# Second feed-forward matmul of a fused block: five groups by seven products and one plain, two groups interleaved, differences of activations formed in the first matmul

## Chip, cores and metric

The kernel runs on one core of one Trainium2 chip. The metric is the device time of one execution in microseconds (us). Before the change the median of three runs is 813.99 us (813.52 to 814.81).

## What is computed

One layer of a hybrid encoder block on 512 positions of 1024 features. The part that matters here is its end, the feed-forward network (in the kernel everything is float32, and every product of two float32 matrices is made of three TensorE matmuls on high and low parts):

```
xn = modulate(rmsnorm(h, norm2_g[l]), sh2, sc2)
ff = jnp.square(jax.nn.relu(xn @ w_ff1[l])) @ w_ff2[l]     # 512x1024 @ 1024x4096, then 512x4096 @ 4096x1024
h = h + g2[:, None, :] * ff
...
return rmsnorm(h, final_g)
```

## The kernel before, in words

**Tiles.** The hidden activations (after squared ReLU) stay in SBUF, feature-major, in tiles `hq[n, nh, th]` of 128 partitions x 512 elements: group `n` of 512 hidden features (8 groups), half `nh` of its features, half `th` of the 512 positions. In the code `a11 = hq[n,0,0]`, `a12 = hq[n,1,0]`, `a21 = hq[n,0,1]`, `a22 = hq[n,1,1]`. The second weight matrix comes in tiles of 128 x 1024 (512 KB): `F11`, `F21` (left half of the output features) through the feed `left`, `F12`, `F22` (right half) through the feed `right` (class `Feed`, L1041). Each feed has a fixed number of buffers: three for `left`, four for `right`. SyncE (SP) issues every load, in order, and a load waits until its buffer is free (L1053).

**Products.** The first matmul (L1013 to L1030) works on groups 1 to 7 with seven products each; a product there is 24 matmuls of 256 columns. The second matmul takes groups 0 to 5 in products (a product: 12 matmuls of 512 columns), and the last 8 of the 32 blocks of 128 features plainly (L1242 to L1259, 192 matmuls). `GROUPS = "WWSWWS"` says which of the six groups is of kind W (seven products, Winograd's form of Strassen's scheme) and which of kind S (eight plain products). The products run in two passes over the six groups: in the first a W group gives P1, P2, P7, P3 and an S group P2, P3, P2, P3; in the second a W group P5, P6, P4 and an S group P4, E, P4, E. That makes 24 + 20 = 44 products, numbered 0 to 43 here. P1 and P2 need tiles of `left` only; P7 and P3 are the first to need `right`. The accumulators take all eight PSUM banks, and `after` (L1171) adds them into SBUF tiles at products 20, 25 and 41.

**Operands.** Each product needs its weights split into high and low parts (`w_pair`, L1068: a ScalarE cast, L1075, and a VectorE subtraction, L1076, both on 128 x 1024) and its activations split (`hl`, L1084: ScalarE L1092, VectorE L1093, 128 x 512). A W group also needs differences of weights (VectorE, 128 x 1024: L1106, L1114, L1118, L1122) and of activations (VectorE, 128 x 512: `S3 = a11 - a21` in a tile of its own, L1105, then L1108 to L1110 in place). `passes` (L1096) is a generator that emits this work; `prefetch_step(5)` (L1197) keeps it five products ahead in program order. Split weights lie in five buffers, three of a pool that the first matmul uses too and two (`wx`) in the pool `passes`.

**Order.** The program order is a priority: a scheduler puts each engine's instructions in a fixed order ahead of time and may move one up into time in which it expects the engine to be free. The pools for `wx`, for `right` and for the split activations from the third on (`hsp`) take the room of the first matmul's operands, and so open only when its last product is done (L1143 to L1151). The first instruction that SyncE issues behind that point is the load of `fing` (L1147), the final norm's weights broadcast to all partitions, needed only at L1268. `gated` (L1165, two VectorE instructions a call) multiplies results by `g2` and adds them to the residual: quarter "1" at product 29 (L1209), the others through the list `late` (L1221) in the plain part, two calls per block.

Of the kernel before, what the change touches and what calls it, by code (L numbers as in the profile page):

```python
# [8 lines left out]
F32 = mybir.dt.float32  # L9
# [40 lines left out]
def block_kernel(ctx, tc, vecs_d, rows_d, ws_d, x_d, w_ada, w_in, w_out, w_ff1, w_ff2, out_d):  # L50
# [961 lines left out]

    for n in range(1, NB):  # L1013
# [16 lines left out]
        relu2(c12, c12)  # L1030

    GROUPS = "WWSWWS"
# [63 lines left out]
    def passes():  # L1096
        for pas in range(2):
            for n, kind in enumerate(GROUPS):
                a11, a12, a21, a22 = hq[n, 0, 0], hq[n, 1, 0], hq[n, 0, 1], hq[n, 1, 1]
                if kind == "W" and pas == 0:  # L1100
                    yield hl(a11), w_pair(left.get(), left)
                    yield hl(a12), w_pair(left.get(), left)
                    b12, b22 = right.get(), right.get()
                    s3 = fp.tile([P, 2, 256], F32, tag="tmp", name=f"S3{n}", bufs=2)
                    dve.tensor_sub(out=s3, in0=a11, in1=a21)  # L1105
                    dve.tensor_sub(out=b12, in0=b22, in1=b12)  # L1106
                    yield hl(s3), w_pair(b12, right)
                    dve.tensor_add(out=a21, in0=a21, in1=a22)  # L1108
                    dve.tensor_sub(out=a11, in0=a21, in1=a11)
                    dve.tensor_sub(out=a12, in0=a12, in1=a11)  # L1110
                    yield hl(a12), w_pair(b22, right)
                elif kind == "W":
# [3 lines left out]
                    yield hl(a21), w_pair(b12)  # L1116
# [3 lines left out]
                    yield hl(a11), w_pair(b22)  # L1120
# [10 lines left out]
    plan_ = [(pas, key) for pas in range(2) for kind in GROUPS for key in later(kind, pas)]  # L1131
# [15 lines left out]
    sp.dma_start(out=fing, in_=rows_d[5].partition_broadcast(P))  # L1147
# [48 lines left out]
    for i, (pas, key) in enumerate(plan_):  # L1196
        prefetch_step(5)  # L1197
        (h_, l_), (wh, wl) = ready.pop(0)
        first = (key, 0) not in acc_b
        for t in range(2):  # L1200
            if first:
                acc_b[key, t] = bank(f"g{key}{t}")
            ts_ = slice(t * P, (t + 1) * P)
            for j in range(2):
                mm3(acc_b[key, t], h_[:, j, ts_], l_[:, j, ts_], wh[:, j], wl[:, j], first and j == 0,
                    i == last_of[key] and j == 1 and key not in ("P4", "E"))
        for key_ in jobs.get(i, ()):
            after(key_)
        if i == end0 + 6:  # L1209
            for t in range(2):  # L1210
                gated("1", t, t, 0)
        if NS - i <= 4:
            ws_ff.prefetch(max(0, 4 - (NS - i)))
        if i == NS - 2:
            hs_pair(KF // 2)
# [5 lines left out]
    late = [(nm, t, row + t, hf) for nm, row, hf in (("3", 0, 1), ("7", 2, 0), ("5", 2, 1)) for t in range(2)]  # L1221
# [105 lines left out]
```

## Time and profile before

| | us |
|---|---|
| median of three runs | 813.99 |
| the profiled execution, its own time | 815.62 |
| its span, first to last instruction | 813.8 |
| TensorE busy | 795.4 (98%) |
| VectorE busy | 615.3 (76%) |
| ScalarE busy | 404.1 (50%) |
| mean granted TensorE clock | 0.994 of full speed |

The span is 1.8 us shorter than the execution's time. Busy TensorE counts modelled ends of pipelined matmuls: a matmul of 512 columns is shown as 0.39 us, while the next one starts 0.23 us after it. Likewise VectorE instructions overlap a little, so that the distance from start to start is what an instruction costs in a queue.

### The profile page before, as it was taken

How to read it: one execution, taken by the hardware profiler on the slowest of the kernel's cores; microseconds unless marked ns; L12 is line 12 of the kernel's file. 1: busy time of each engine (PE TensorE's matmuls, PEld its weight loads, DVE VectorE, ACT ScalarE, POOL GpSimd, SP SyncE). 2: the span in 40 equal slices, each digit the busy share in tenths (PEclk: the TensorE clock that was granted, in tenths of full speed). 3: DMA queues.
4: the chain of work that ended last, by engine and by line, in shares of the span. 5: the costliest groups of instructions: out<-in, count | busy, mean ns of one | idle time of the engine just before them, and what ended most of it. 6: DMA issues, size and time to landing. Idle time of an engine off the chain costs nothing.

```text
span 813.8 us, 11472 instructions
## 1 busy us (share of the span) xinstructions
PE 795.4 (98%) x4375; PEld 689.1 (85%) x4375; DVE 615.3 (76%) x925; ACT 404.1 (50%) x606; POOL 43.0 (5%) x62
## 2 busy tenths in 40 slices
PE   7999999999999999999999999999999799999996
PEld 6787888888988888888888899999999688888885
DVE  5889667684834367988756689988888898998936
ACT  5457556274432333242443446666666665555414
POOL 2004020121100000100000100000000000000000
PEclk9999999999999999999999999999999999999999
DMA  8974331143233398577345241333331676774302
GB/s 271 264 224 126 114 101 45 27 135 99 79 103 82 108 352 283 154 254 272 126 137 200 78 131 52 104 105 104 105 104 52 221 244 203 236 224 138 125 6 103
DMA packets 76423, 119.87 MB, mean 147 GB/s; under 512 B 5712, under 2 KB 38608, under 8 KB 76368
## 3 DMA queue, kind: packets, MB, share of 16 engines
q1 hardware_dynamic: 76368, 119.14, 46.0%
q8 instruction: 34, 0.56, 0.3%
q14 instruction: 21, 0.17, 0.1%
HBM read 117.02 MB, written 2.10 MB: 146 GB/s over the span
## 4 chain that ended last, share of the span: by engine, by line
PE 93%; DMA 2%; SPq 1%; ACT 1%; issue 1%; DVE 1%; POOLq 0%; POOL 0%
PE P L119 6%; PE P L117 6%; PE P L118 6%; PE gP L117 5%; PE gP L118 5%; PE gP L119 5%; PE qk L282 4%; PE wo L117 2%; PE wo L119 2%; PE wo L118 2%; PE f10b L118 1%; PE f10b L117 1%; PE f10b L119 1%; PE k1b L117 1%; PE o0b L119 1%
## 5 line engine op out<-in xcount | busy, mean ns | idle before, releaser
L1092 ACT CAST hsh<-h 128x512 fp32r<-128x512 f32 x38 | 23.6, 621 | 35.3 <-PE gP L118 27.2
L117 PE MATMUL gP<-wh_g,hsh 128*128 128x512 f32 x92 | 36.2, 396 | 0.2 <-ACT wh_g L1075 0.2
L118 PE MATMUL gP<-wl_g,hsh 128*128 128x512 f32 x92 | 35.8, 389 | 0.0
L119 PE MATMUL gP<-wh_g,hsl 128*128 128x512 f32 x92 | 35.8, 389 | 0.0
L1075 ACT CAST wh_g<-F 128x1024 fp32r<-128x1024 f32 x27 | 28.2, 1049 | 13.7 <-issue 7.1
L1076 DVE TENSOR_TENSOR wl_g<-F,wh_g 128x1024 fp32r<-128x1024 f32 x27 | 32.9, 1222 | 2.6 <-ACT wh_g L1075 2.5
L921 ACT CAST wh_T<-T 128x1024 fp32r<-128x1024 f32 x21 | 22.0, 1048 | 20.8 <-PE P L118 19.1
L118 PE MATMUL P<-x2l,wh_B 128*128 128x256 f32 x112 | 31.6, 282 | 0.0
L117 PE MATMUL P<-x2h,wh_B 128*128 128x256 f32 x112 | 31.6, 282 | 0.0
L119 PE MATMUL P<-x2h,wl_B 128*128 128x256 f32 x112 | 31.6, 282 | 0.0
L921 ACT CAST wh_B<-B 128x1024 fp32r<-128x1024 f32 x21 | 22.0, 1048 | 16.4 <-PE P L118 15.4
L1093 DVE TENSOR_TENSOR hsl<-h,hsh 128x512 fp32r<-128x512 f32 x38 | 25.9, 688 | 4.6 <-ACT hsh L1092 4.6
L117 PE MATMUL gP<-wh_x,hsh 128*128 128x512 f32 x60 | 23.8, 400 | 4.8 <-ACT wh_x L1075 4.8
L922 DVE TENSOR_TENSOR wl_T<-T,wh_T 128x1024 fp32r<-128x1024 f32 x21 | 25.7, 1224 | 2.6 <-ACT wh_T L921 2.5
L922 DVE TENSOR_TENSOR wl_B<-B,wh_B 128x1024 fp32r<-128x1024 f32 x21 | 25.6, 1220 | 0.0
L96 DVE TENSOR_TENSOR wl_gb<-raw_gb,wh_gb 128x1024 fp32r<-128x1024 f32 x8 | 9.8, 1224 | 19.7 <-ACT wh_gb L95 19.6
L118 PE MATMUL gP<-wl_x,hsh 128*128 128x512 f32 x60 | 23.7, 396 | 0.0
L119 PE MATMUL gP<-wh_x,hsl 128*128 128x512 f32 x60 | 23.6, 393 | 0.0
L667 DVE SCALAR_TENSOR_TENSOR accg<-arg,c_act,accg 128x1024 f32<-128x1024 f32 x14 | 18.0, 1283 | 5.6 <-DMA arg<-in_w_ada 5.5
L95 ACT CAST wh_ga<-raw_ga 128x1024 fp32r<-128x1024 f32 x8 | 8.4, 1051 | 27.2 <-PE ga0b L119 16.3
L1076 DVE TENSOR_TENSOR wl_x<-F,wh_x 128x1024 fp32r<-128x1024 f32 x17 | 20.7, 1222 | 1.4 <-ACT wh_x L1075 1.4
L118 PEld LDWEIGHTS P<-x2l,wh_B 128*128 128x128 f32 x112 | 21.3, 191 | 0.0
(610 smaller groups left out, 2815.5 us busy)
## 6 DMA issues: line engine op xcount, KB each, us to landing
F<-in_w_ff SPq DMA_DIRECT2D x48, 512.0 KB, 4.2
B<-in_w_ff SPq DMA_DIRECT2D x28, 512.0 KB, 3.8
ar<-in_w_ada SPq DMA_DIRECT2D x64, 128.0 KB, 3.4
arg<-in_w_ada SPq DMA_DIRECT2D x16, 512.0 KB, 5.9
raw_f<-in_w_ff SPq DMA_DIRECT2D x12, 512.0 KB, 3.3
raw_o<-in_w_in SPq DMA_DIRECT2D x8, 512.0 KB, 4.2
raw_mv<-in_w_in SPq DMA_DIRECT2D x8, 512.0 KB, 3.6
raw_gb<-in_w_in SPq DMA_DIRECT2D x8, 512.0 KB, 3.6
```

The source lines that it names most:

```text
L96: dve.tensor_sub(out=wl, in0=raw, in1=wh.bitcast(F32))
L117: pe.matmul(out, lhsT=ah, rhs=bh, start=start, stop=False)
L118: pe.matmul(out, lhsT=ah, rhs=bl, start=False, stop=False)
L119: pe.matmul(out, lhsT=al, rhs=bh, start=False, stop=stop)
L282: pe.matmul(bk, lhsT=wx[:, kk, f * P:(f + 1) * P], rhs=xx[k], start=k == 0 and ps_ == 0, stop=k == KT - 1 and ps_ == 2)
L667: dve.scalar_tensor_tensor(out=acc, in0=raw, scalar=c_act[:, k:k + 1], in1=acc, op0=ALU.mult, op1=ALU.add)
L921: act.copy(out=wh, in_=src)
L922: dve.tensor_sub(out=wl, in0=src, in1=wh.bitcast(F32))
L1075: act.copy(out=wh, in_=src)
L1076: dve.tensor_sub(out=wl, in0=src, in1=wh.bitcast(F32))
L1092: act.copy(out=h_, in_=src)
L1093: dve.tensor_sub(out=l_, in0=src, in1=h_.bitcast(F32))
```

## The change

The diff does the following. Group 2 becomes a W group (`GROUPS = "WWWWWS"`), which gives 43 products. The first pass begins with P1, P2 of group 0 and P1, P2 of group 1, then P7, P3 of both; the later groups keep their order. `a21` is replaced by `a11 - a21` beside the first matmul (`minus_a21`, one VectorE instruction for each of the five W groups), and the other differences of the activations are rewritten for it: three in the second matmul in place of four. The load of `fing` moves from the start of the second matmul to the last product of the first pass (`end0`, product 23). The `gated` calls of quarter "1" move into `late`.

```diff
@@ -1010,6 +1010,13 @@
         prefetch_op(2)
         return bk.rearrange("p (f t) -> p f t", f=2)
 
+    GROUPS = "WWWWWS"
+
+    def minus_a21(n):
+        if GROUPS[n:n + 1] == "W":
+            dve.tensor_sub(out=hq[n, 0, 1], in0=hq[n, 0, 0], in1=hq[n, 0, 1])
+
+    minus_a21(0)
     for n in range(1, NB):
         c = {(nh, th): ring(f"h{n}{nh}{th}") for nh in range(2) for th in range(2)}
         for key, v in c.items():
@@ -1028,8 +1035,8 @@
         relu2(c21, c21)
         dve.tensor_add(out=c12, in0=c12, in1=product(sum_op("S4"), f"P3{n}"))
         relu2(c12, c12)
-
-    GROUPS = "WWSWWS"
+        minus_a21(n)
+
     NF = len(GROUPS)
     NK = FF // P
     KF = 4 * NF
@@ -1094,30 +1101,32 @@
         return h_, l_
 
     def passes():
+        for n in range(2):
+            for nh in range(2):
+                yield hl(hq[n, nh, 0]), w_pair(left.get(), left)
         for pas in range(2):
             for n, kind in enumerate(GROUPS):
                 a11, a12, a21, a22 = hq[n, 0, 0], hq[n, 1, 0], hq[n, 0, 1], hq[n, 1, 1]
                 if kind == "W" and pas == 0:
-                    yield hl(a11), w_pair(left.get(), left)
-                    yield hl(a12), w_pair(left.get(), left)
+                    if n > 1:
+                        yield hl(a11), w_pair(left.get(), left)
+                        yield hl(a12), w_pair(left.get(), left)
                     b12, b22 = right.get(), right.get()
-                    s3 = fp.tile([P, 2, 256], F32, tag="tmp", name=f"S3{n}", bufs=2)
-                    dve.tensor_sub(out=s3, in0=a11, in1=a21)
                     dve.tensor_sub(out=b12, in0=b22, in1=b12)
-                    yield hl(s3), w_pair(b12, right)
-                    dve.tensor_add(out=a21, in0=a21, in1=a22)
-                    dve.tensor_sub(out=a11, in0=a21, in1=a11)
-                    dve.tensor_sub(out=a12, in0=a12, in1=a11)
+                    yield hl(a21), w_pair(b12, right)
+                    dve.tensor_sub(out=a21, in0=a22, in1=a21)
+                    dve.tensor_sub(out=a12, in0=a12, in1=a21)
+                    dve.tensor_add(out=a11, in0=a21, in1=a11)
                     yield hl(a12), w_pair(b22, right)
                 elif kind == "W":
                     b11, b12 = left.get(), right.get()
                     dve.tensor_sub(out=b12, in0=b12, in1=b11)
                     left.more()
-                    yield hl(a21), w_pair(b12)
+                    yield hl(a11), w_pair(b12)
                     b22 = right.get()
                     dve.tensor_sub(out=b22, in0=b22, in1=b12)
                     right.more()
-                    yield hl(a11), w_pair(b22)
+                    yield hl(a21), w_pair(b22)
                     b21 = left.get()
                     dve.tensor_sub(out=b21, in0=b21, in1=b22)
                     right.more()
@@ -1128,7 +1137,9 @@
                         yield x_, w_pair(left.get(), left)
                         yield x_, w_pair(right.get(), right)
 
-    plan_ = [(pas, key) for pas in range(2) for kind in GROUPS for key in later(kind, pas)]
+    plan_ = [(0, key) for key in ("P1", "P2") * 2 + ("P7", "P3") * 2]
+    plan_ += [(0, key) for kind in GROUPS[2:] for key in later(kind, 0)]
+    plan_ += [(1, key) for kind in GROUPS for key in later(kind, 1)]
     gen = passes()
     ready = []
 
@@ -1144,7 +1155,6 @@
     mhs.close()
     hsp = ff.enter_context(tc.tile_pool(name="hsp", bufs=1, side="right"))
     fing = hsp.tile([P, D], F32, name="fing")
-    sp.dma_start(out=fing, in_=rows_d[5].partition_broadcast(P))
     ps_stack = ExitStack()
     pass_pool.append(ps_stack.enter_context(tc.tile_pool(name="passes", bufs=1, side="right")))
     for _ in range(4):
@@ -1206,9 +1216,8 @@
                     i == last_of[key] and j == 1 and key not in ("P4", "E"))
         for key_ in jobs.get(i, ()):
             after(key_)
-        if i == end0 + 6:
-            for t in range(2):
-                gated("1", t, t, 0)
+        if i == end0:
+            sp.dma_start(out=fing, in_=rows_d[5].partition_broadcast(P))
         if NS - i <= 4:
             ws_ff.prefetch(max(0, 4 - (NS - i)))
         if i == NS - 2:
@@ -1218,7 +1227,7 @@
     lwp = ff.enter_context(tc.tile_pool(name="lwp", bufs=1, side="right"))
     o_banks = [[bank(f"ob{t}{hf}") for hf in range(2)] for t in range(2)]
     o_banks += [[acc_b["P4", t], acc_b["E", t]] for t in range(2)]
-    late = [(nm, t, row + t, hf) for nm, row, hf in (("3", 0, 1), ("7", 2, 0), ("5", 2, 1)) for t in range(2)]
+    late = [(nm, t, row + t, hf) for nm, row, hf in (("1", 0, 0), ("3", 0, 1), ("7", 2, 0), ("5", 2, 1)) for t in range(2)]
 
     def ff2_piece(k, last=False):
         if last:
```

## Rows read from the trace of the kernel before

**Rows 1.** The page of the profile: the line of busy times (engine, busy us, share of the span, instructions) and the first line of the chain that ended last.

```profile
PE 795.4 (98%) x4375; PEld 689.1 (85%) x4375; DVE 615.3 (76%) x925; ACT 404.1 (50%) x606; POOL 43.0 (5%) x62
...
PE 93%; DMA 2%; SPq 1%; ACT 1%; issue 1%; DVE 1%; POOLq 0%; POOL 0%
```

**Rows 2.** Waits of TensorE in the stretch 560 to 815 us: who waited for whom, us in total, times, longest. These are all it has there.

```profile
PE gP L117 <- ACT wh_x L1075: 4.8, 1, 4.8
...
PE gP L117 <- ACT wh_g L1075: 0.2, 1, 0.2
```

**Rows 3.** Table by stretches of the second feed-forward matmul (us from the span's start: length, busy us and instructions of PE, weight loads, DVE, ACT, POOL; granted clock; DMA share; GB/s).

```profile
641.60:646.50 4.90, 0.19 (x1) 0.00 (x0) 3.45 (x5) 1.99 (x3) 0.00 (x0) 1.00 0.77 295
...
651.00:702.00 51.00, 51.00 (x226) 42.24 (x226) 44.99 (x51) 30.46 (x38) 0.00 (x0) 1.00 0.68 225
...
702.00:762.70 60.70, 60.70 (x269) 50.26 (x269) 56.77 (x67) 31.11 (x38) 0.00 (x0) 1.00 0.56 179
```

**Rows 4.** The same table in stretches of 1 us behind the pause.

```profile
648.00:649.00 1.00, 1.00 (x4) 0.71 (x3) 1.00 (x2) 0.92 (x2) 0.00 (x0) 0.50 0.84 238
...
651.00:652.00 1.00, 1.00 (x6) 0.80 (x6) 1.00 (x3) 0.43 (x1) 0.00 (x0) 1.00 0.96 340
```

**Rows 5.** Timeline of TensorE (start us, length, engine, line, operation, tiles; in brackets the idle time before it): the first matmul of product 0, the last one before the pause, the first one behind it, the first and the last matmul of the plain part (192 matmuls).

```profile
636.16 0.40 PE L117 MATMUL gP<-wh_g,hs 128*128 128x512 f32 x1
...
641.40 0.39 PE L119 MATMUL gP<-wh_g,hs 128*128 128x512 f32 x1
...
646.55 0.77 PE L117 MATMUL gP<-wh_x,hsh 128*128 128x512 f32 x2 [4.76 <-ACT wh_x L1075]
...
762.81 0.39 PE L117 MATMUL ob<-wh_f,hsh 128*128 128x512 f32 x1
...
806.10 0.39 PE L119 MATMUL gE<-wh_f,hsl 128*128 128x512 f32 x1
```

**Rows 6.** The chain of waits of the stretch 600 to 700 us, in order of time (start us, us, what).

```profile
636.36 0.84 SPq L1147
...
637.25 7.24 DMA F<-in_w_ff
...
644.51 1.35 ACT wh_x L1075 x2
...
646.41 1.05 ACT wh_g L1075
```

**Rows 7.** Timeline of SyncE's queue: the last load issued before that of `fing`. Then the transfers issued in two short stretches, of that load (635.6 to 635.8 us) and of `fing` (636.2 to 636.4 us); the last number is us from issue to landing.

```profile
635.74 0.37 SPq L1053 DMA_DIRECT2D F<-in_w_ff  x1
...
F<-in_w_ff SPq DMA_DIRECT2D x1, 512.0 KB, 4.8
...
fing<-in_rows SPq DMA_DIRECT2D x1, 512.0 KB, 6.8
```

**Rows 8.** Timeline of VectorE around the pause.

```profile
640.03 0.68 DVE L1093 TENSOR_TENSOR hsl<-h,hsh 128x512 fp32r<-128x512 f32 x1
...
640.63 0.69 DVE L1093 TENSOR_TENSOR hsl<-S,hsh 128x512 fp32r<-128x512 f32 x1
...
644.58 1.22 DVE L1106 TENSOR_TENSOR F<-F,F 128x1024 f32<-128x1024 f32 x1 [1.45 <-DMA F<-in_w_ff]
...
650.26 1.22 DVE L1106 TENSOR_TENSOR F<-F,F 128x1024 f32<-128x1024 f32 x1
...
651.39 0.69 DVE L1093 TENSOR_TENSOR hsl<-h,hsh 128x512 fp32r<-128x512 f32 x1
```

**Rows 9.** Groups of instructions by line in 636.2 to 763 us (shapes, count, busy us, mean ns of one, idle before and its releaser): three of VectorE, one of ScalarE.

```profile
L1076 DVE TENSOR_TENSOR wl_g<-F,wh_g 128x1024 fp32r<-128x1024 f32 x25 | 30.5, 1222 | 2.3 <-ACT wh_g L1075 2.2
...
L1093 DVE TENSOR_TENSOR hsl<-h,hsh 128x512 fp32r<-128x512 f32 x32 | 21.9, 688 | 4.6 <-ACT hsh L1092 4.6
...
L1114 DVE TENSOR_TENSOR F<-F,F 128x1024 f32<-128x1024 f32 x4 | 4.9, 1223 | 0.5 <-DMA F<-in_w_ff 0.5
...
L1075 ACT CAST wh_g<-F 128x1024 fp32r<-128x1024 f32 x25 | 26.1, 1049 | 11.8 <-issue 7.1 <-DVE F L1106 2.7 <-PE gP L119 2.1
```

**Rows 10.** The end of the first feed-forward matmul: the table by stretches for 600 to 636.2 us; the first matmul of two products that follow each other on TensorE; and VectorE's split of an operand in that time.

```profile
600.00:636.20 36.20, 36.20 (x308) 36.20 (x308) 30.57 (x34) 23.53 (x31) 0.00 (x0) 1.00 0.24 74
...
613.44 0.28 PE L117 MATMUL P<-S4hl,wh_B 128*128 128x256 f32 x1
...
616.28 0.28 PE L117 MATMUL P<-x2h,wh_B 128*128 128x256 f32 x1
...
614.61 1.23 DVE L922 TENSOR_TENSOR wl_T<-T,wh_T 128x1024 fp32r<-128x1024 f32 x1 [0.21 <-ACT wh_T L921]
```

**Rows 11.** Timeline of VectorE in the second pass: the first difference of weights for product 24, the split of the weights for product 30, and the only wait of this stretch.

```profile
687.89 1.22 DVE L1114 TENSOR_TENSOR F<-F,F 128x1024 f32<-128x1024 f32 x1
...
715.87 1.22 DVE L1076 TENSOR_TENSOR wl_g<-F,wh_g 128x1024 fp32r<-128x1024 f32 x1
...
718.21 1.23 DVE L1114 TENSOR_TENSOR F<-F,F 128x1024 f32<-128x1024 f32 x1 [0.52 <-DMA F<-in_w_ff]
```

**Rows 12.** Timeline of VectorE at the end of the plain part: the last split of weights, and the next instruction.

```profile
775.27 1.23 DVE L1230 TENSOR_TENSOR wl_f<-raw_f,wh_f 128x1024 fp32r<-128x1024 f32 x1 [0.26 <-ACT wh_f L1229]
...
787.49 0.69 DVE L1261 TENSOR_TENSOR ot<-ob,rowg 128x512 f32<-128x512 f32 x1 [11.00 <-PE ob L119]
```

## The prediction

> **What bounds the kernel now.** I read the page first: TensorE is busy for 98% of the span and holds 93% of the chain that ended last [rows 1]. So an instruction less on TensorE is worth its time, and an instruction on another engine is worth something only where TensorE waits for it. Next the waits of TensorE in the last 255 us, which hold the end of the first feed-forward matmul and all of the second: two waits in one place, 4.8 and 0.2 us, both for a ScalarE cast of weights [rows 2]. The reader should see that TensorE waits nowhere else there. The timeline gives the place: product 0 begins at 636.16, the matmuls of products 0 and 1 end with the one begun at 641.40, and the next begins at 646.55 [rows 5]. The chain of waits names what was late: SyncE issued `fing` at 636.36, the next load at 637.25, that load took 7.24 us, and ScalarE's cast of it began at 644.51 [rows 6]. It is a tile of `right`, which P7 and P3 of group 0 need. Last the table by stretches: behind the pause the granted clock was 0.50 of full speed (1.2 of 2.4 GHz) in the microsecond from 648, and 1.00 again from 651 [rows 4]; in the long stretches from 651 on it is 1.00 and TensorE is full [rows 3]. It fell after TensorE had stood still for 4.9 us.
>
> **Units.** The plain part is 192 matmuls from 762.81 to 806.10 with no wait: 43.29 / 191 = 0.2266 us each, so a product of 12 costs 2.72 us. VectorE needs 1.13 us from start to start for a 128 x 1024 instruction (650.26 to 651.39) and 0.60 for a 128 x 512 one (640.03 to 640.63) [rows 8]; the durations shown are 1.22 and 0.69 [rows 9]. All sums are made against the profiled execution, 815.62 us with a span of 813.8; it lies 1.63 above the median of the runs shown, and I carry the difference over to the median, 813.99.
>
> **Part 1, group 2 by seven products.** It removes one product: 12 matmuls, 2.72 us, all on the path. VectorE's and ScalarE's part is below.
>
> **Part 2, two groups together.** Four products that need only `left` (0 to 3) now stand ahead of the first that needs `right`. They start at 636.16, 638.88, 641.60 and 644.32, and P7 of group 0 is due at 647.04 in place of 641.63. Are products 2 and 3 in time? The last tile that product 3 needs comes no later than the load issued at 635.74, landed 4.8 us later, 640.5 [rows 7]; with a cast of 1.05 and a split of 1.22 [rows 9] it is ready at 642.8, 1.5 us early. Is P7? Its tile landed at 644.5 [rows 6]. With a difference (1.13), a cast (1.05) and a split (1.22) behind it, it would be ready at 647.9, 0.9 us late. That is the upper end, the landing being as before. The lower end: `fing` no longer stands ahead. It landed 6.8 us after 636.36, at 643.2, and the load ahead of it at 640.5, so it held the queue for up to 2.7 us [rows 6, 7]; 2.7 us earlier, P7 is ready at 645.2 and waits for nothing. I take 0.3 us, nearer to the lower end because the transfer ahead is really gone. The Trainium skill, "DMA: Bandwidth & Descriptors", section "Queues, rings and completion order", says that each DMA engine consumes a ring's descriptors in order. By that rule the tile comes 2.7 us earlier, the 0.3 is 0, and the time 0.3 us less than the one I give.
>
> VectorE's time up to 647.04 is 10.6 us from the end of the first matmul. In it fall two splits, a difference and a split of weights (4 x 1.13) and some four activation instructions (4 x 0.60), 6.9 us. So the queue has room. The pause of 641.63 to 646.55 goes: 4.92 us. With it goes what the clock cost. From 646.55 to 762.81 TensorE ran 42 products, 504 x 0.2266 = 114.21 us, in 116.26: 2.05 us too long, all of it behind the pause (the 0.2 of the second wait is in it) [rows 2 to 5]. A wait of under 1 us should not bring the low clock back: the granted clock still read 1.00 through the pause itself [rows 3].
>
> **Part 3, VectorE.** Group 2 as W instead of S adds, in the second matmul, three activation splits (0.60), four weight differences (1.13) and, with the four old in-place differences per W group becoming three, one activation difference less in all (16 to 15), and it removes one weight split (1.13): +1.8 + 4.5 - 0.6 - 1.1 = +4.6 us. Where does it fall? A first-pass W group now costs VectorE 4 splits of weights, 4 of activations, one difference of weights, three of activations: 5 x 1.13 + 7 x 0.60 = 9.9 us, against 4 x 2.72 = 10.9 on TensorE: room. A second-pass W group costs 6 x 1.13 + 3 x 0.60 = 8.6 against 3 x 2.72 = 8.2: VectorE loses 0.42 a group, 2.1 in five, and the `after` work for P3 and P2 (4 x 0.60) makes it 4.5. What covers it is VectorE's lead. The split for product 30 was done at 717.1 [rows 11], while TensorE began product 30 at 762.81 - 14 x 2.72 = 724.7, 7.6 us later, although two W groups and `after` lay just before. It also runs differences ahead: the first one of pass 2, for product 24, stood at 687.89 [rows 11], when TensorE was at product 16. So I cost it at nothing on the path. If the lead were gone, the price is at most the 4.5 us. ScalarE has a cast less and three small ones more and is far from full [rows 1].
>
> **Part 4, five instructions in the first matmul.** 5 x 0.60 = 3.0 us of VectorE, where it stands idle for 5.6 us of 36.2 [rows 10]. Each waits for ScalarE's squared ReLU, and operand splits queue behind it. The split begun at 614.61 ended at 615.84; TensorE began a product at 616.28, 2.84 after the last, and needs this operand for the one after, at 619.12 [rows 10]: 3.3 us of cover, more than 0.60 plus a wait for two ScalarE instructions. Cost 0; without the cover 0.60 a group.
>
> **Part 5, what is moved.** `fing` goes behind the right-hand loads, which gain up to 2.7 us (counted above), and ahead of second-pass loads, which lose as much. VectorE waited for a load there once, 0.52 us [rows 11]; with 7.6 us of lead TensorE does not see 2.7 more. Its issue takes SyncE 0.84 us [rows 6], which the same lead covers. The `gated` calls move 4 x 0.60 = 2.4 us of VectorE out of the second pass into the plain part, where VectorE's last split ended at 776.5 and it then stood idle for 11.0 us [rows 12]. Cost 0. What follows the last matmul stays as it is.
>
> **Sum.** 2.72 + 4.92 + 2.05 - 0.3 = 9.4 us. The profiled execution would take 806.2, the median 804.6.
>
> **Rivals.**
> - *The pause moves to P7 and keeps part of its size.* For: four products are 10.9 us of cover and the tile landed 8.3 us after product 0, so 2.5 us are left for a difference, a cast and a split in series. If the scheduler puts two loads of `left` ahead of the right-hand ones, they come 2.6 us later (1.3 each, as the tile of [rows 6] landed 1.3 behind `fing`): a wait of 3.5 us, and with the 2.05 of the clock 813.99 - 9.7 + 5.5 = 809.8. Against: the buffers of `left` are full until product 2's weights are split, some 3 us behind the right-hand loads.
> - *VectorE is short in five W groups in a row*, without a fall of the clock: up to 4.5 us, 804.3 + 4.5 = 808.8. For: 8.6 against 8.2. Against: the lead.
> - *The order does not take effect*: the scheduler, which places by its own forecast, keeps group 0's P7 early. Only the product is won: 811.3. Against: P7's operand cannot be there before 644, and a forecast that kept P7 early would have to ignore that load.
> - *Slower: the pause comes back in the second pass.* There each of the five W groups has three weight splits that each wait for a difference and a cast. If loads arrive late there, five pauses like the one removed can appear, each with its clock loss. Two such (2 x 6.97 = 13.9) would eat more than the gain: 804.3 + 13.9 = 818.2. It decides against the change from 9.7 us of pauses and clock loss on. Against: no wait of TensorE behind 651, with W groups in pairs. The Trainium skill, "TensorE: Matmul & The Clock Gate", section "A second HAM failure mode: psum-queue depth-cycling", tells of a kernel whose short idle times between groups of matmuls sent the clock back and forth. By that, waits shorter than the one removed would be enough here; no row before shows it.
>
> **Numbers.** About 0.2% (1.6 us) is what a measurement of this kernel can tell from no change. Forecast as summed 0.70; pause at P7 0.12; VectorE short 0.09; order without effect 0.04; pauses in the second pass 0.05. The predicted time is 804.6. Its own spread is 803.6 to 805.5 (the 0.3 between 0 and 0.9, and the runs' spread of 0.8). The range goes below it to 803.2, the runs having spread by 0.5 downward, and up to 808.5, taking in most of the second and third cases. Faster 0.95 (the first four cases); of the last 0.05, 0.01 for pauses that just eat the gain and 0.04 for slower.
>
> **What would show it.** Right: on TensorE no wait over 1 us around 641 or 647, granted clock 1.00 in every stretch from 636 on, the last product's end 9 to 10 us earlier, 43 casts of weights, and a lead of VectorE in the second pass that shrinks but stays positive. Wrong: a wait for a cast or a split at P7 of group 0, waits on VectorE's weight splits between products 24 and 38, or waits in the first matmul behind `minus_a21`.

## The result, and the profile after

The changed kernel takes 806.1 us (median of four runs, 804.74 to 806.75) where the kernel before takes 814.4 beside it: a ratio of 0.9891, 95% interval 0.9872 to 0.991, so 8.9 us less (7.3 to 10.4; the two medians lie 8.3 apart). Measured again with experiments on another occasion it took 805.48, ratio 0.9884 (0.9867 to 0.99). The profiled execution took 806.75 with a span of 805.0; before 815.62 and 813.8, so 8.87 less. The forecast was 9.4 less and 804.6.

**A measure that scatters less.** Product 0 begins anywhere from 634.3 to 636.7 us in executions of these kernels, whatever is changed behind it. I therefore use the *stretch*: from the first matmul of product 0 to the last of the plain part. Before it is 806.10 - 636.16 = 169.94 us [rows 5]. Without any pause it would hold n - 1 steps of 0.2266 us: 162.93 for 44 products and the plain part (719 steps), 160.21 for 43, 157.49 for 42. What is above that I call the *excess*: 7.0 us before.

**After.** The timeline of TensorE: the first matmul of product 0, the place of the only wait, the first and the last matmul of the plain part.

```profile
636.13 0.40 PE L117 MATMUL gP<-wh_g,hs 128*128 128x512 f32 x1
...
649.98 0.39 PE L118 MATMUL gP<-wl_g,hsh 128*128 128x512 f32 x1
650.78 0.50 PE L119 MATMUL gP<-wh_g,hsl 128*128 128x512 f32 x1 [0.41 <-DVE hsl L1100]
651.12 0.39 PE L117 MATMUL gP<-wh_g,hsh 128*128 128x512 f32 x1
...
753.95 0.39 PE L117 MATMUL ob<-wh_f,hsh 128*128 128x512 f32 x1
...
797.24 0.39 PE L119 MATMUL gE<-wh_f,hsl 128*128 128x512 f32 x1
```

The stretch is 161.11 us, the excess 0.90. Beside [rows 5] the reader sees that the pause at 641.40 is gone, and that a small wait stands one product later than the prediction put it: not at P7 of group 0 (product 4, which begins at 647.03, as computed), but in P3 (product 5), whose third matmul starts 0.80 us after the second, 0.57 too late. The plain part takes 43.29 us, as before.

The waits of TensorE from 560 to 806 us, all of them (compare [rows 2]):

```profile
PE gP L119 <- DVE hsl L1100: 0.4, 1, 0.4
```

The table by stretches (columns as in [rows 3]):

```profile
641.60:646.50 4.90, 4.90 (x23) 4.08 (x22) 4.55 (x5) 2.11 (x2) 0.00 (x0) 1.00 0.97 352
646.50:651.00 4.50, 4.09 (x19) 3.08 (x18) 4.50 (x7) 3.64 (x5) 0.00 (x0) 1.00 0.90 313
651.00:702.00 51.00, 51.00 (x225) 42.04 (x225) 50.97 (x62) 30.62 (x42) 0.00 (x0) 1.00 0.68 220
702.00:754.00 52.00, 52.00 (x231) 43.03 (x230) 51.51 (x60) 27.55 (x36) 0.00 (x0) 1.00 0.56 181
```

TensorE is full, and the granted clock is 1.00 everywhere. The new thing is the third busy figure, VectorE: 50.97 of 51.00 and 51.51 of 52.00, where it had 44.99 of 51 and 56.77 of 60.7 [rows 3].

The chain of waits from 635 to 651 us, in order of time (start us, us, what; "issue" is time in which the engine waited for nothing shown):

```profile
635.71 0.37 SPq L1060
636.12 5.73 DMA F<-in_w_ff
642.04 1.05 issue
643.09 0.68 DVE hsl L1100
643.77 0.81 DVE wl_g L1083
644.58 0.25 issue
644.83 1.22 DVE wl_x L1083
646.04 0.60 DVE h L1117
646.72 0.98 issue
647.70 0.68 DVE h L1118
648.38 0.60 DVE h L1119
648.99 1.14 DVE wl_x L1083
650.12 0.61 DVE hsl L1100
650.78 0.50 PE gP L119
```

The tile of `right` in this chain is the second of the two (`F12`, `F22`) that the difference for P7 of group 0 takes. The first is issued ahead of it, before the change even ahead of `fing` (at 633.90, landed at 639.2), so `fing` is not quite the first load behind that point. The second landed 8.3 us after product 0 began in [rows 6]; here it is issued at 636.12 and lands at 641.85, 5.7 us after product 0 begins. From there on the chain runs through VectorE.

### The profile page after: what moved, and what is told of

The parts are those of the page before. It is cut to its first block, busy times and chain, and to the rows that moved or that the text cites. A ratio compares the mean times of both kernels' runs of the same rounds, so it can differ in the third digit from the quotient of the medians.

```text
span 805.0 us, 11450 instructions
## 1 busy us (share of the span) xinstructions
PE 792.6 (98%) x4363; PEld 687.5 (85%) x4363; DVE 620.6 (77%) x935; ACT 403.6 (50%) x608; POOL 43.0 (5%) x62
## 4 chain that ended last, share of the span: by engine, by line
PE 94%; DVE 2%; DMA 1%; issue 1%; ACT 1%; SPq 0%; POOL 0%; POOLq 0%; DVEq 0%
PE P L119 6%; PE P L117 6%; PE P L118 6%; PE gP L119 4%; PE gP L117 4%; PE gP L118 4%; PE qk L282 4%; PE wo L117 2%; PE wo L119 2%; PE wo L118 2%; PE cp L241 1%; PE f10b L118 1%; PE f10b L117 1%; PE f10b L119 1%; PE k1b L117 1%
## 5 line engine op out<-in xcount | busy, mean ns | idle before, releaser
L1099 ACT CAST hsh<-h 128x512 fp32r<-128x512 f32 x45 | 26.7, 620 | 26.8 <-PE gP L118 15.4
L1100 DVE TENSOR_TENSOR hsl<-h,hsh 128x512 fp32r<-128x512 f32 x45 | 29.6, 681 | 0.3 <-ACT hsh L1099 0.3
L976 ACT ACTIVATE h<-h 128x512 f32<-128x512 f32 x28 | 17.7, 631 | 8.4 <-DVE h L1036 4.0
L1082 ACT CAST wh_x<-F 128x1024 fp32r<-128x1024 f32 x16 | 16.6, 1049 | 9.7 <-DVE F L1115 3.9
L119 PEld LDWEIGHTS P<-x2h,wl_B 128*128 128x128 f32 x112 | 21.3, 190 | 0.0
```

What stands on the lines that cost most here:

```text
L119: pe.matmul(out, lhsT=al, rhs=bh, start=False, stop=stop)
L976: act.activation(dst, src, AF.Relu)
L1082: act.copy(out=wh, in_=src)
L1099: act.copy(out=h_, in_=src)
L1100: dve.tensor_sub(out=l_, in0=src, in1=h_.bitcast(F32))
```

## The experiments

The theory: the excess is one late tile of `right`, the pause while TensorE waits for it, and the low clock behind that pause; two more products that need only `left` cover it, the seventh product less is worth its 2.72 us, and nothing else in the change matters. The rivals: most of the gain comes from `fing` standing out of the way; the slow microseconds behind the pause come from something else than the clock; the differences formed in the first matmul carry part of the gain. A landing is told below as the time from the start of product 0 to the landing of that late tile, the second one of `right`. Each ratio is to runs of the kernel before on the same occasion, whose medians were 814.4, 815.25 and 815.34 us, so it is the ratios that compare, not the medians of the table. Stretch and excess are those of one profiled execution each.

| kernel | median us | ratio to before (95%) | stretch us | excess us |
|---|---|---|---|---|
| before (profiled: 815.62) | 814.4 | 1 | 169.94 | 7.0 |
| the change | 806.1 | 0.9891 (0.9872 to 0.991) | 161.11 | 0.90 |
| the change, again | 805.48 | 0.9884 (0.9867 to 0.99) | 161.28 | 1.07 |
| order alone | 808.97 | 0.9914 (0.9894 to 0.9933) | 165.21 | 2.28 |
| order alone, again (one run) | 809.29 | | 164.17 | 1.24 |
| group 2 by seven alone | 812.94 | 0.9971 (0.9955 to 0.9988) | 167.91 | 7.70 |
| pause filled | 813.85 | 0.9982 (0.997 to 0.9994) | 169.14 | 6.21 |
| `fing` alone | 813.34 | 0.9965 (0.9951 to 0.998) | 167.26 | 4.33 |
| the change, `fing` back | 806.36 | 0.9894 (0.9878 to 0.991) | 161.32 | 1.11 |
| the change, differences back | 806.08 | 0.9887 (0.9868 to 0.9905) | 160.99 | 0.78 |
| the change, one addition later | 806.04 | 0.9894 (0.9873 to 0.9914) | 161.43 | 1.22 |
| six groups by seven | 805.38 | 0.9884 (0.9864 to 0.9905) | 160.55 | 3.06 |
| differences on GpSimd | 817.98 | 1.0043 (1.0027 to 1.006) | 173.74 | 13.5 |
| six groups, differences on GpSimd | 821.86 | 1.0081 (1.0067 to 1.0096) | 176.39 | 18.9 |

**1. The order alone**, in the kernel before: only the first four products and the plan are changed.

```diff
     def passes():
+        for n in range(2):
+            for nh in range(2):
+                yield hl(hq[n, nh, 0]), w_pair(left.get(), left)
...
-    plan_ = [(pas, key) for pas in range(2) for kind in GROUPS for key in later(kind, pas)]
+    plan_ = [(0, key) for key in ("P1", "P2") * 2 + ("P7", "P3") * 2]
+    plan_ += [(0, key) for kind in GROUPS[2:] for key in later(kind, 0)]
+    plan_ += [(1, key) for kind in GROUPS for key in later(kind, 1)]
```

> The kernel before with one edit: P1 and P2 of groups 0 and 1 stand ahead of P7 and P3 of both; 44 products, old differences, fing at its old place. Measure: from the first matmul of product 0 to the last matmul, 169.94 us before and 161.11 after. Theory (the pause is the right-hand tile landing late, two products of cover being too few, and the low clock comes from the pause): the pause of 4.92 and the 2.05 of clock go, 163.0, or up to 163.9 where P7 waits for the tile behind fing; ratio of times about 0.992. Rival (fing's place in the queue makes the pause, and the order alone leaves most of it): 165 or more.

Measured: ratio 0.9914, excess 2.28: 4.7 of the 7.0 us are gone with `fing` still ahead. Two short waits are left, both in product 4 (P7 of group 0):

```profile
648.37 0.73 PE L117 MATMUL gP<-wh_x,hsh 128*128 128x512 f32 x2 [0.58 <-ACT wh_x L1075]
...
650.16 0.50 PE L118 MATMUL gP<-wl_x,hsh 128*128 128x512 f32 x1 [1.06 <-DVE wl_x L1076]
```

This is the wait that the prediction feared at P7. The first part is for the cast behind the late tile. The second is for the split of the same weights, which VectorE begins at 648.89, behind the split for product 5 (647.15) and a difference of activations (648.29). In this execution the tile landed 9.2 us after product 0, later than in the execution of before (8.3): the issue of `fing` took SyncE 1.30 us, and `fing` landed 3.0 us behind the load ahead of it. To see whether the wait follows the landing, I ran it once more:

> The kernel of order_only once more, for a second profile. In its first profile fing's transfer held the queue for 3.0 us and the right-hand tile landed 9.2 us behind product 0; in fing_back, with the same order of loads on SyncE, they were 1.5 and 7.4. Theory (how long the broadcast load of fing holds the queue differs from execution to execution): 1.5 to 3.0 us again, and the excess over unbroken matmuls (2.27 us) follows the landing: below 1 us where the tile lands 7.5 us behind product 0, 2 us where it lands 9. Rival (the old differences and the plain group 2 make the excess): 2.2 us wherever the tile lands.

Measured: landing 8.1, excess 1.24, and one wait of 0.8 us. An earlier tile, a smaller wait: the 1.07 us by which the landings differ come back as 1.04 us of excess.

**2. Group 2 by seven products alone**, `GROUPS = "WWWWWS"` in the kernel before.

> The kernel before with one edit: GROUPS WWWWWS, so 43 products in the old order with the old differences. Theory: one product less is worth its 12 matmuls, 2.72 us, and the pause stays as it was: 167.2 us from product 0 to the last matmul, ratio about 0.9965. Rival (VectorE is short with five W groups in a row): new waits of TensorE on VectorE in the second pass, 168 us or more.

Measured: ratio 0.9971; the stretch is 2.03 us shorter. The product's 2.72 are there, but the pause was longer in this execution (the tile landed 9.0 after product 0), so the excess is 7.70:

```profile
645.61 1.22 PE L117 MATMUL gP<-wh_x,hsh 128*128 128x512 f32 x2 [5.43 <-ACT wh_x L1075]
```

It is the only wait of TensorE from 560 us on. VectorE's 5.7 us more (621.0 busy against 615.3) cost nothing.

**3. The pause filled with work.** In the kernel before, 20 matmuls on operands that are there stand ahead of product 2; they write the accumulator that product 2's first matmul overwrites, so they add nothing to the result.

```diff
+            if i == 0:
+                h0 = h_
+            if i == 2 and t == 0:
+                for _ in range(20):
+                    pe.matmul(acc_b[key, t], lhsT=h0[:, 0, 0:P], rhs=h0.rearrange("p a b -> p (a b)"),
+                              start=True, stop=True)
```

> The kernel before with 20 matmuls of 512 columns more, behind product 1, on operands already there and into a bank that product 2 overwrites: they fill the pause and add nothing that is used. Theory (the 2.05 us behind the pause are the clock's, which fell because TensorE stood still): granted clock 1.00 from 647 on, the pause keeps its length but the stretch falls from 169.94 to about 167.9 us. Rival (the slow stretch behind the pause is operands that arrive late, or the added matmuls delay the real ones): 169.9 or more.

Measured: the timeline of TensorE, the 20 matmuls and then the first product that needs `right`; and the table by stretches behind them.

```profile
639.75 4.70 PE L1208 MATMUL gP<-hs 128*128 128x512 f32 x20
645.57 0.73 PE L117 MATMUL gP<-wh_g,hsh 128*128 128x512 f32 x2 [1.13 <-ACT wh_g L1075]
```

```profile
645.60:650.00 4.40, 4.40 (x19) 3.42 (x20) 4.40 (x5) 1.75 (x3) 0.00 (x0) 1.00 0.79 236
```

The product starts 5.82 us later than without the pause, nearly a microsecond worse than before: TensorE's order begins here with weights (`wh_g`) that ScalarE casts third behind the landing, where before it began with the second (`wh_x`). And yet the kernel is 1.5 us faster (0.9982): behind the resumption 0.4 us are lost in all, where before lost 2.05. The clock stayed at 1.00 in every stretch, where [rows 4] has 0.50. So all but some 0.4 us of the slow stretch behind the pause are the clock's, not those of a load or a queue: shown.

**4. `fing` alone**: its load moved to product 23 in the kernel before.

```diff
-    sp.dma_start(out=fing, in_=rows_d[5].partition_broadcast(P))
...
+        if i == end0:
+            sp.dma_start(out=fing, in_=rows_d[5].partition_broadcast(P))
```

> The kernel before with one edit: the load of fing is written at product 23. The scheduler puts it behind the four right-hand loads. Theory (loads of one queue land in the order of issue): the right-hand tile lands up to 2.7 us earlier, at 641.8, the pause shrinks from 4.9 to 2.2 us, and a shorter pause may keep the clock up: 165.2 to 167.2 us from product 0 to the last matmul. Rival (transfers in flight share the engines, so that the order of issue matters little): pause and stretch as before, 169.9.

Measured: ratio 0.9965; the excess falls by 2.7 us, to 4.33. The pause is halved, and what is left of it still costs the clock (timeline of TensorE, and the table by stretches):

```profile
644.77 1.22 PE L117 MATMUL gP<-wh_x,hsh 128*128 128x512 f32 x2 [2.48 <-ACT wh_x L1075]
```

```profile
644.80:649.00 4.20, 4.20 (x12) 3.16 (x13) 4.20 (x5) 1.81 (x2) 0.00 (x0) 0.63 0.63 199
```

The start is 2.63 us late; 4.33 - 2.63 = 1.7 us are lost behind it, almost as much as behind the pause of 4.9.

**5. The change with `fing` back in its old place.**

> The kernel after with one edit: the load of fing is written at its old place, ahead of the right-hand loads. Measure: from the first matmul of product 0 to the last one, 161.11 us after. Theory (the move of fing is what lets the right-hand tile land 5.8 us behind product 0 and P7 start without a wait): the tile lands some 9 us behind product 0, P7 and P3 of group 0 wait about 2 us in all, as they did with the new order and the old place of fing (excess of 2.3 us over unbroken matmuls): 162.4 to 163.5. Rival (the new order alone suffices, the prediction's upper bound): 161.1 to 161.9.

Measured: excess 1.11 against 0.90 and 1.07 of the change; ratios 0.9894 and 0.9891. The tile landed 7.4 us after product 0, not 5.7, and neither P7 nor P3 of group 0 waited; one wait of 0.2 us stands at 655.01. So with the order in place, moving `fing` is worth at most some 0.2 us in these executions. It is not additive: it shortens the same wait that the order covers. How much it insures in an execution with a late landing (9.2, experiment 1) stays open; no such execution of this kernel was seen.

**6. The change with the old differences**: no `minus_a21`, `S3` formed in the second matmul again.

```diff
-        if GROUPS[n:n + 1] == "W":
+        if False:
             dve.tensor_sub(out=hq[n, 0, 1], in0=hq[n, 0, 0], in1=hq[n, 0, 1])
...
+                    s3 = fp.tile([P, 2, 256], F32, tag="tmp", name=f"S3{n}", bufs=2)
+                    dve.tensor_sub(out=s3, in0=a11, in1=a21)
                     dve.tensor_sub(out=b12, in0=b22, in1=b12)
-                    yield hl(a21), w_pair(b12, right)
-                    dve.tensor_sub(out=a21, in0=a22, in1=a21)
-                    dve.tensor_sub(out=a12, in0=a12, in1=a21)
-                    dve.tensor_add(out=a11, in0=a21, in1=a11)
+                    yield hl(s3), w_pair(b12, right)
+                    dve.tensor_add(out=a21, in0=a21, in1=a22)
+                    dve.tensor_sub(out=a11, in0=a21, in1=a11)
+                    dve.tensor_sub(out=a12, in0=a12, in1=a11)
...
```

> The kernel after with one edit: no difference formed in the first matmul; the old four differences for each group in the second one, S3 in a tile of its own. Theory (VectorE is the next bound from product 4 on: it runs without a break from 643 us and its order decides): the wait of P3 of group 0, 0.6 us, grows by one or two instructions of 0.60: 161.6 to 162.9. Rival (VectorE has room, as the prediction costed it): 161.1.

Measured: stretch 160.99, excess 0.78, ratio 0.9887. Forming the differences beside the first matmul neither costs nor gains anything that can be measured. The one wait, 0.4 us at 707.32, is for VectorE's reading of an accumulator in `after` (L1191). Nor do the differences in the first matmul buy VectorE lead: the split for product 38 is done 3.6 us before TensorE begins it here (735.6 and 739.2), against 1.1 in the change.

**7. One addition later.** The wait at P3 stands behind VectorE's instructions; `a11 + a21` is needed only in the second pass, so I put it behind groups 3 and 4 for groups 0 and 1.

```diff
-                    dve.tensor_add(out=a11, in0=a21, in1=a11)
+                    if n > 1:
+                        dve.tensor_add(out=a11, in0=a21, in1=a11)
                     yield hl(a12), w_pair(b22, right)
+                    if n in (3, 4):
+                        m = n - 3
+                        dve.tensor_add(out=hq[m, 0, 0], in0=hq[m, 0, 1], in1=hq[m, 0, 0])
```

> The kernel after with one edit: the sum a21 + a11 of groups 0 and 1, which only the second pass needs, is formed behind the products of groups 3 and 4 instead of ahead of P3's split. Theory (the one wait that is left is P3 of group 0 waiting behind VectorE instructions that are not yet needed): one instruction of 0.60 ahead of that split goes, the wait of 0.4 us goes: 160.3 to 160.6 us. Rival (the wait has another cause, or the scheduler fills the place with another instruction): 161.1.

Measured: nothing is won (excess 1.22, one wait of 0.7 us in the same place). VectorE's timeline there:

```profile
645.04 1.22 DVE L1115 TENSOR_TENSOR F<-F,F 128x1024 f32<-128x1024 f32 x1
646.18 0.68 DVE L1118 TENSOR_TENSOR h<-h,h 128x512 f32<-128x512 f32 x1
646.78 0.68 DVE L1124 TENSOR_TENSOR h<-h,h 128x512 f32<-128x512 f32 x1
647.38 1.22 DVE L1083 TENSOR_TENSOR wl_x<-F,wh_x 128x1024 fp32r<-128x1024 f32 x1
648.52 1.28 DVE L1100 TENSOR_TENSOR hsl<-h,hsh 128x512 fp32r<-128x512 f32 x2
```

The scheduler moved the addition (now L1124) up into the same place, so the edit did not take effect. The queue is the scheduler's, not the program order's.

**8. Six groups by seven products**: how much of VectorE is left? `GROUPS = "WWWWWW"`, and new banks in the plain part in place of those of E, which no group computes now; 42 products.

```diff
-    GROUPS = "WWWWWS"
+    GROUPS = "WWWWWW"
...
-    o_banks += [[acc_b["P4", t], acc_b["E", t]] for t in range(2)]
+    o_banks += [[acc_b["P4", t], bank(f"oE{t}")] for t in range(2)]
...
-        mm3(o_banks[t][hf], h_, l_, wh[:, 0, cs], wl[:, 0, cs], k == KF and t < 2, stop)
+        mm3(o_banks[t][hf], h_, l_, wh[:, 0, cs], wl[:, 0, cs], k == KF and (t < 2 or hf == 1), stop)
```

> The kernel after with group 5 by seven products too: 42 products, no plain group, and the last two accumulators start in the plain part. Theory (TensorE is the bound and VectorE keeps its lead through six W groups): 12 matmuls less, 158.4 us from product 0 to the last matmul. Rival (VectorE is the bound by now, since the plain group was where it caught up, 5.8 us of VectorE against 10.9 of TensorE): waits of TensorE on VectorE in the second pass or ahead of the plain part eat it, 160.5 us or more.

Measured: 12 matmuls less, 2.72 us, but the stretch is only 0.6 shorter than the change's and the ratio the same (0.9884 against 0.9891 and 0.9884). In the second pass TensorE loses 1.9 us in short waits. Here is the first and longest, in the timeline of TensorE, and behind it the table by stretches.

```profile
704.71 0.61 PE L117 MATMUL gP<-wh_g,hsh 128*128 128x512 f32 x2
705.76 0.50 PE L118 MATMUL gP<-wl_g,hsh 128*128 128x512 f32 x1 [0.43 <-DVE wl_g L1083]
```

```profile
651.00:702.00 51.00, 51.00 (x227) 42.05 (x226) 51.00 (x63) 30.85 (x43) 0.00 (x0) 1.00 0.65 208
702.00:753.00 51.00, 50.54 (x217) 39.82 (x216) 50.65 (x56) 27.70 (x36) 0.00 (x0) 1.00 0.58 187
```

VectorE is busy for 101.65 of 102.00 us, and TensorE waits for its splits: the bound has moved to it. (The busy share alone would not tell: the change has 102.48 of 103.00 there and no such waits.) The five groups of the change are as far as this goes without work being taken off VectorE.

**9. The differences of the activations on GpSimd**, which is idle there, with five groups and with six.

```diff
-                    dve.tensor_sub(out=a21, in0=a22, in1=a21)
-                    dve.tensor_sub(out=a12, in0=a12, in1=a21)
-                    dve.tensor_add(out=a11, in0=a21, in1=a11)
+                    pool.tensor_tensor(out=a21, in0=a22, in1=a21, op=ALU.subtract)
+                    pool.tensor_tensor(out=a12, in0=a12, in1=a21, op=ALU.subtract)
+                    pool.tensor_tensor(out=a11, in0=a21, in1=a11, op=ALU.add)
```

> The kernel after with one edit: the three differences of activations per W group of the second matmul run on GpSimd, which is idle there; 15 instructions of 0.60 us leave VectorE. Theory (the 0.9 us that the five W groups leave over unbroken matmuls are VectorE's queue): excess 0 to 0.3 us, 160.2 to 160.5 us from product 0 to the last matmul. Rival (GpSimd is slow or late at three instructions in a row, and P3's split waits for it instead): 161.1 or more.

> The kernel six_w with the same edit: 42 products, and 18 differences of activations on GpSimd. In six_w TensorE waited some 3 us in all on VectorE from product 24 on, and 160.55 us came out against 157.5 unbroken (707 - 12 matmuls of 0.2266). Theory (VectorE was the bound there): 10.8 us less on VectorE, 157.5 to 158.5 us, the fastest of the kernels here, some 2.5 us faster than after. Rival (GpSimd's own time or the last accumulators bound it): 160 or more.

Measured: both are slower than the kernel before, 1.0043 and 1.0081. With five groups, the groups of instructions from 636 us to the plain part: GpSimd's three, and VectorE's weight splits beside them.

```profile
L1117 POOL TENSOR_TENSOR h<-h,h 128x512 f32<-128x512 f32 x5 | 11.0, 2209 | 182.2 <-DVE hsl L1100 182.2
L1118 POOL TENSOR_TENSOR h<-h,h 128x512 f32<-128x512 f32 x5 | 9.0, 1809 | 0.4
L1119 POOL TENSOR_TENSOR h<-h,h 128x512 f32<-128x512 f32 x5 | 7.5, 1493 | 0.0
...
L1083 DVE TENSOR_TENSOR wl_g<-F,wh_g 128x1024 fp32r<-128x1024 f32 x25 | 33.1, 1327 | 0.8 <-ACT wh_g L1082 0.8
```

An instruction that takes VectorE 0.69 us [rows 9] takes GpSimd 1.5 to 2.2 on average; the mean of VectorE's own weight splits grows from 1.22 to 1.33 us. ScalarE's casts wait 20.2 us in all for L1118, and TensorE for the splits behind them. Of the 13.5 us of excess 6.4 are six late starts of 0.2 to 2.4 us, 3.7 a longer one, behind VectorE's late reading of an accumulator, and 1.8 the low clock behind that one. The chain from difference to split is what counts, and it got longer.

**10. The change once more**, on the occasion of these runs.

> The kernel after once more, beside the two above: a second profile and times on the same chip. Expected 161.1 us from product 0 to the last matmul within 0.4, one wait of TensorE on VectorE near product 5, and a ratio of about 0.989.

Measured: excess 1.07, one wait at P3, 0.71 us late. The wait at P3 is no accident of one execution.

No version here beats the change by more than the runs can tell: six groups and the old differences lie inside its interval.

## Why the prediction was right, step by step

- **What bounds it: right.** One pause of one late tile. The order alone takes away 4.7 to 5.8 of the 7.0 us of excess, and the two kernels without the order but with `fing` or group 2 changed keep a pause.
- **The product, 2.72: right.** 43 products fill 160.21 us of the stretch; alone it gave 2.03, the other 0.7 went into a longer pause of that execution. The last product ends 8.9 us earlier (the plain part begins at 753.95, before at 762.81), just outside the 9 to 10 that the prediction named as a sign.
- **The pause, 4.92, and the clock, 2.05: right in kind and size.** The excess went from 7.0 to 0.90. That all but some 0.4 of the 2.05 are the clock's was argued in the prediction and is shown by the filled pause.
- **The wait left over, 0.3: in the wrong place and too small.** P7 waited for nothing: the tile came at the lower bound (5.7 us behind product 0), the end that the rule of ring order in the Trainium skill, "DMA: Bandwidth & Descriptors", section "Queues, rings and completion order", stood for in the prediction; this trace agrees with it. The seven loads of weights issued from 635.71 to 644.94 landed in the order of their issue, 1.3 to 1.4 us apart. P7's split ended at 646.05, 1.0 us early and not 1.8 as the lower bound had it, mainly since VectorE did the split for product 5 first. The step that failed is the list of VectorE's work up to 647.04: it holds what P7 needs and ends there. P3, one product later, has a chain of its own: two differences in series (L1117, L1118), a cast, a split. And the scheduler filled VectorE with work for later:

```profile
644.83 1.22 DVE L1083 TENSOR_TENSOR wl_x<-F,wh_x 128x1024 fp32r<-128x1024 f32 x1
645.96 0.68 DVE L1117 TENSOR_TENSOR h<-h,h 128x512 f32<-128x512 f32 x1
646.57 1.22 DVE L1115 TENSOR_TENSOR F<-F,F 128x1024 f32<-128x1024 f32 x1
647.70 0.68 DVE L1118 TENSOR_TENSOR h<-h,h 128x512 f32<-128x512 f32 x1
648.30 0.68 DVE L1119 TENSOR_TENSOR h<-h,h 128x512 f32<-128x512 f32 x1
648.90 1.22 DVE L1083 TENSOR_TENSOR wl_x<-F,wh_x 128x1024 fp32r<-128x1024 f32 x1
650.04 1.28 DVE L1100 TENSOR_TENSOR hsl<-h,hsh 128x512 fp32r<-128x512 f32 x2
```

  This is VectorE's timeline after. The last line is the split that P3 waits for. Ahead of it stand L1115 (1.13 us, group 1's difference), L1119 (0.60, needed in the second pass) and the split at 648.90 (1.14, into the buffer that product 3 had just left, for product 8): 2.9 us that could have come later (part of it fills the time of the cast from 648.42 to 649.04), and the wait is 0.57. The term came to 0.9 in place of 0.3, and 9.4 to 8.8, which is what the stretch lost (169.94 - 161.11 = 8.83). With the tile at its real landing the prediction's own list would have given 0; that the term came out within its bounds, at the upper one, is luck. The rest of the way from 804.6 to 806.1 is 0.4 us of a slower kernel before in the same runs and the scatter between executions.
- **The upper bound of that term was too low.** It was 0.9, with the tile landing as in the one execution of before. The experiments that keep `fing` ahead saw landings from 7.4 to 9.2 us after product 0, and the order alone left an excess of 2.28, of which the late landing makes one part and VectorE's order the other (experiment 1). A bound that rests on one transfer of one execution is no bound.
- **VectorE's 4.6 us at nothing: right, with less to spare than it sounded.** The lead in the second pass is nearly gone: the split of product 38's weights ends at 739.3 and product 38 begins at 740.35, about 1 us later, where product 30 had 7.6 before. These are VectorE's and TensorE's rows:

```profile
738.07 2.35 DVE L1083 TENSOR_TENSOR wl_x<-F,wh_x 128x1024 fp32r<-128x1024 f32 x2
...
740.35 0.39 PE L117 MATMUL gP<-wh_x,hsh 128*128 128x512 f32 x1
```

  Six groups spend it. "Shrinks but stays positive" was right by a microsecond.
- **The differences in the first matmul at nothing: right**, both ways (experiment 6).
- **`fing` ahead of second-pass loads: wrong, and harmless.** The scheduler does not wait for product 23:

```profile
646.53 0.42 SPq L1220 DMA_DIRECT2D fing<-in_rows  x1
```

  It is issued at once when the loads ahead of it are out, with TensorE in product 3, some 53 us before product 23 begins, and no wait of TensorE comes of it. That it goes behind the first loads of `right` was the part that mattered.
- **`gated` at nothing: right.** The plain part takes 43.29 us with the eight instructions in it, and behind its last split of weights VectorE still stands idle for 6.6 us (11.0 in [rows 12]).
- **The rivals.** The pause at P7, VectorE short and the order without effect did not happen. The slower rival, pauses with clock loss in the second pass, did not either; differences on GpSimd show what it would look like. The prediction cited the Trainium skill, "TensorE: Matmul & The Clock Gate", section "A second HAM failure mode: psum-queue depth-cycling", for short idle times that send the clock back and forth; in these runs waits of 0.2 to 1.1 us, repeated in the six-group kernel, left the granted clock at 1.00. Waits shorter than the one removed were enough all the same: 2.48 us of idle time with `fing` alone, 1.85 in the six-group kernel with differences on GpSimd (last section).

## What to carry to other kernels

Where one late transfer makes a pause, look first for work that needs none of it and put that ahead; hastening the transfer shortens the same wait and does not add to it. When a wait is moved, list the producer's queue up to the product *after* the one that you rescue too, with whatever a scheduler may pull forward into it. And price an engine that fills up by its lead at the last point where it is needed, not by its share of busy time: this one went from 7.6 us of lead to 1 with a change that looked free, and the next product saved was worth a quarter of its size.

## What the runs showed of the hardware

- **The clock's price hardly depends on the length of the pause, and the length alone does not decide whether it is paid.** Behind starts that were 2.63 us (`fing` alone), 3.7 (differences on GpSimd), 4.92 (before) and 5.59 late (group 2 alone), 1.7, 1.8, 2.05 and 2.0 us more were lost. In the six-group kernel with differences on GpSimd it was 1.7, 1.6 and 1.8 us behind starts 2.02, 2.24 and 3.0 late. Yet behind a start 2.37 us late in that same execution 0.1 was lost and the granted clock read 1.00, and the same behind one 2.44 late, at 653.90, with five groups. What sets these apart the runs do not tell. Here are two starts of one execution, the first without the price and the second with it: TensorE's rows, and the table by stretches behind them.

```profile
655.51 0.50 PE L118 MATMUL gP<-wl_g,hsh 128*128 128x512 f32 x1 [2.21 <-DVE wl_g L1083]
690.61 0.50 PE L118 MATMUL gP<-wl_g,hsh 128*128 128x512 f32 x1 [1.85 <-DVE wl_g L1083]
```

```profile
655.50:660.00 4.50, 3.65 (x14) 2.53 (x15) 2.71 (x3) 3.36 (x5) 2.36 (x2) 1.00 0.50 166
690.60:695.00 4.40, 4.39 (x12) 3.52 (x13) 4.40 (x4) 4.40 (x7) 1.10 (x1) 0.61 0.41 137
```

- **GpSimd and VectorE slow each other.** A difference of 128 x 512 on GpSimd took from 1.29 us, with VectorE idle (677.12), to 3.28, beside two of VectorE's instructions that took 1.21 each (673.76). The other way round, a split begun at 643.51 beside one on GpSimd took 2.31 us; splits with none beside them took 1.22. In both cases the one that began later ended about 1.1 us behind the other. The Trainium skill, "GPSIMD Engine Reference", section "Specifications", says that GpSimd shares its SBUF interfaces with VectorE, with contention where a VectorE instruction has two SBUF inputs; the splits have two, and the trace agrees. With 1.5 to 2.2 us on average against 0.69 it is no spare VectorE beside a busy one.
- **What a load costs the queue depends on where it stands.** `fing`, a row broadcast to 128 partitions and 512 KB as the other loads are, landed 1.5 to 3.0 us behind the load ahead of it in six executions with it in its old place. In the eight where it goes behind the first loads of `right` the distance was 1.25 to 1.33, that of a plain load [rows 6]. So it is not the broadcast that costs, and what does stays open. Nor is its slow issue its own: it took SyncE 0.34 to 1.30 us in the old place, and with `fing` elsewhere a plain load there took up to 1.39.
